# A recurrence with one PSUM bank per pair of heads, r-times-state beside U, and the state carried on VectorE

## The chip, the cores and the metric

The kernel runs on one core of a Trainium2 chip. The metric is device time in microseconds (us) of one execution, the median of several. One core has a matrix engine (TensorE, "PE" in the profile, with its weight loads as "PEld"), VectorE ("DVE"), ScalarE ("ACT"), GpSimd ("POOL") and SyncE ("SP"), which here issues the transfers. Matrix products write to PSUM, which has eight banks of 2 KiB per partition; VectorE and ScalarE read it from there.

## The reference, cut to what matters

One decoder layer: RMSNorm with modulation, one input projection, an RWKV-7 time-mixing group (8 heads of 64), a latent-attention group (8 heads), gates, an output projection, a final RMSNorm. SEQ is 1024, D_MODEL 1024, everything in f32. The change concerns the recurrence of the time-mixing group alone:

```python
def rwkv7_scan(r, w, k, v, kk, a):
    def step(state, inp):
        r_t, w_t, k_t, v_t, kk_t, a_t = inp
        sa = jnp.einsum('bhvk,bhk->bhv', state, kk_t)
        state = (state * w_t[:, :, None, :]
                 - sa[..., None] * (kk_t * a_t)[:, :, None, :]
                 + v_t[..., None] * k_t[:, :, None, :])
        y = jnp.einsum('bhvk,bhk->bhv', state, r_t)
        return state, y
    s0 = jnp.zeros((B, H, N, N), jnp.float32)
    _, ys = lax.scan(step, s0, xs)
    return jnp.moveaxis(ys, 0, 1)
```

## The kernel before

The tokens are cut into 16 chunks of 64. Inside a chunk the recurrence is written with matrices; from chunk to chunk a 64 x 64 state per head is handed on. Heads are taken in pairs: two heads share the 128 partitions (64 rows each, index `s`), and two pairs (index `a`) are worked on together, so a group of four heads has 16 chunks one after the other, and there are two such groups. Four chunks of a group make a *unit*; there are eight units, 0 to 3 for the first group and 4 to 7 for the second.

For each unit, `prep`, `products`, `invert`, `fetch` and `tmat` make the matrices: `GA` (the products of keys and queries inside a chunk, for U and for the outputs), `TT` (the inverse of a triangular matrix, whose 31 steps of two operations each run on VectorE, lines L625 and L627), `KB` (keys, turned), `rq` (queries scaled by decays) and `eL` (the decay over a whole chunk). `chain` then runs the recurrence, chunk by chunk, with three stages for each chunk, separated by `yield`:

1. X: four products of `GA` with `ST` (L694) into PSUM, and a ScalarE copy to `X` (L697). `ST` holds, for each chunk and head, the state in one half of the partitions and the values v in the other.
2. U: four products of `TT` with `X` (L701), and two ScalarE operations that write -U in the place of the state in `ST` (L703, L704).
3. State and output. State: for each pair an identity product with the old state `Sv` (L709) and a product of `KB` with `ST` on top of it (L712) in the same PSUM place; then ScalarE scales the sum by `eL` and writes it four times into the next chunk's `ST` (L720) and twice into `Sn` (L722). Output: a product of `rq` with the old state (L725) and one of `GA` with `ST` on top (L728), into `Y`.

X, U and next state of both pairs lie in one bank (tag `rc`), the outputs `Y` of all four chunks in another (`ry`). `post` copies `Y` out when the unit is done (L739) and norms, gates and stores it.

The outer loop at the end of the listing walks the units; unit `n` is prepared while `n - 1` is inverted and `n - 2` is in `chain`. `STEPS` gives the number of places for each unit, and every second place runs one stage of `chain`. Between them `filler` puts the input projection's products (`mm3`, lines L164 to L166: three products of 128 x 512 for each contraction tile, `RATE` of these triples per place), and later those of the values. A list scheduler then sets the final order on each engine by priorities and by its own estimate of when an operation can start; `quick` raises the priority of the recurrence's evacuations. Each engine works its queue in that order, and an operation that waits holds up all behind it. A product that reuses a bank, and an evacuation of it, wait for each other.

`acc`, at the start of the kernel, takes six banks for the first three projection tiles, and uses the two banks of `rc` and `ry` for one of them.

Of the kernel before, what the change touches and what calls it, by code (L numbers as in the profile page):

```python
# [17 lines left out]
F32 = mybir.dt.float32  # L18
# [68 lines left out]
def hymba_kernel(ctx: ExitStack, tc: tile.TileContext, x, pos, cols, cst, winit, w_ada, b_gate, w_in, w_lora, w0,  # L87
# [157 lines left out]
    with ExitStack() as s0:  # L245
# [62 lines left out]
        for i in range(4, 8):  # L308
            load_x(i)
        ws.append(load_w(GROUP[2][0], P, st, 3, st))  # L310
        acc = [[(psM if m == 0 else psA).tile([P, HALF], F32, tag=t, name=f"acc{m}{h}", bufs=1 if m == 1 else 2)
                for h, t in enumerate(tags)] for m, tags in enumerate((("mm", "mm"), ("rc", "ry"), ("rt", "rt")))]
# [365 lines left out]
    def chain(un, nxt):  # L678
# [8 lines left out]
        ps = psA.tile([P, 3, 2, C], F32, tag="rc", name="rc", bufs=1)  # L687
        Y = un["Y"] = psA.tile([P, 8, C], F32, tag="ry", name="Y", bufs=1)
        for i in range(4):
            last = i == 3 and nxt is None  # L690
            cc = [a * 4 + i for a in range(2)]
            for a in range(2):
                for s in range(2):
                    T.matmul(ps[rows[s], 0, a, :], lhsT=GA[s][a][:, i, 0:C], rhs=ST[:, cc[a], s, :], start=True, stop=True)  # L694
            X = ch.tile([P, 2, C], F32, tag="X", name="X", bufs=2)
            with quick(un):
                A.copy(X[:], ps[:, 0])  # L697
            yield
            for a in range(2):
                for s in range(2):  # L700
                    T.matmul(ps[rows[s], 1, a, :], lhsT=TT[rows[s], cc[a], :], rhs=X[rows[s], a, :], start=True, stop=True)  # L701
            with quick(un):
                A.mul(ST[lo, i:8:4, 0, :], ps[lo, 1], -1.0)  # L703
                A.mul(ST[hi, i:8:4, 1, :], ps[hi, 1], -1.0)  # L704
            yield
            Sn = None if last else ch.tile([P, 2, C], F32, tag="S", name="S", bufs=2)
            for a in range(0 if last else 2):
                for s in range(2 if Sv else 0):
                    T.matmul(ps[rows[s], 2, a, :], lhsT=ident[rows[s], rows[s]], rhs=Sv[rows[s], a, :],  # L709
                             start=True, stop=False)  # L710
                for s in range(2):
                    T.matmul(ps[rows[s], 2, a, :], lhsT=KB[:, s, cc[a], :], rhs=ST[:, cc[a], s, :],  # L712
                             start=Sv is None, stop=True)
            if not last:

                dst, n = (ST, i + 1) if i < 3 else (nxt["ST"], 0)
                with quick(un):
                    for a in range(2):
                        for s in range(2):
                            A.mul(dst[rows[s], a * 4 + n, s, :], ps[rows[s], 2, a, :], eL[rows[s], cc[a]:cc[a] + 1])  # L720
                    for a in range(2):
                        A.mul(Sn[:, a], ps[:, 2, a], eL[:, cc[a]:cc[a] + 1])  # L722
# [653 lines left out]
```

## Time and profile before

| | us |
|---|---|
| median of 3 runs | 940.63 |
| lowest and highest | 936.82, 945.03 |
| the profiled execution | 940.97 |
| its span, first to last instruction | 939.0 |
| first to last recurrence product | 176 to 628 |

A row of a timeline has start, duration, engine, line, operation, tiles (written <- read) and a count of merged rows. A row of groups has the busy time, the mean time of one in ns, and behind the second bar the idle time of the engine just before and what ended it. In the names of shapes 64\*64 is rows x columns of the weights.

### The profile page before, as it was taken

The page shows a single profiled execution, that of the slowest core. Times are in us where ns is not written, and L with a number is a line of the kernel's source. Part 1 is how long each engine was busy: PE and PEld are TensorE (multiplying, and loading weights), DVE is VectorE, ACT ScalarE, POOL GpSimd, SP SyncE. Part 2 cuts the span into 40 slices and gives each one's busy share as a digit, 9 for nine tenths or more (in the row PEclk, how much of TensorE's full clock was granted, in tenths as well). Part 3 has the DMA queues.
Part 4 walks back from the last instruction along what each step waited for, and adds up shares of the span by engine and source line. Part 5 has one row for each costly group of instructions (what it writes and reads, how often), then busy time and mean ns, then how long its engine had stood idle before and what let it go on. Part 6 is the DMA issues. An engine that isn't in the chain of part 4 may idle for free.

```text
span 939.0 us, 16568 instructions
## 1 busy us (share of the span) xinstructions
PE 852.4 (91%) x5812; PEld 654.2 (70%) x5812; DVE 576.8 (61%) x1462; ACT 477.4 (51%) x1112; POOL 298.7 (32%) x351
## 2 busy tenths in 40 slices
PE   1798997999999999898999999997799998989797
PEld 1586785776777777566777767765678777868685
DVE  5795358376584836747558275266678878763333
ACT  3555231444646545355254564554678888872311
POOL 2311432132222413332151321243346454454300
PEclk9998998999999999997999889989799999999898
DMA  8764443424444434344324443165202121036133
GB/s 266 244 175 146 135 121 102 127 82 118 131 124 98 141 85 136 83 114 148 72 87 119 110 137 101 56 184 157 54 18 72 46 89 48 1 102 214 57 124 123
DMA packets 131714, 106.66 MB, mean 114 GB/s; under 512 B 40616, under 2 KB 108464, under 8 KB 131632
## 3 DMA queue, kind: packets, MB, share of 16 engines
q1 hardware_dynamic: 130672, 102.46, 37.1%
q0 software_dynamic: 960, 3.15, 1.4%
q8 instruction: 46, 0.75, 0.3%
q14 instruction: 36, 0.29, 0.1%
HBM read 76.46 MB, written 29.10 MB: 112 GB/s over the span
## 4 chain that ended last, share of the span: by engine, by line
PE 62%; DVE 14%; ACT 11%; DMA 5%; issue 4%; POOL 2%; SPq 1%; DVEq 0%; POOLq 0%; ACTq 0%
PE mm L164 10%; PE mm L165 8%; PE mm L166 8%; ACT pr L1082 3%; PE gps L577 2%; DMA wor<-in_w_out 2%; DVE wtmp L625 2%; ACT PTh L1102 2%; PE tp L1093 2%; DVE W L627 2%; PE po L1155 2%; PE po L1157 2%; PE po L1156 2%; PE rc L694 1%; PE Y L728 1%
## 5 line engine op out<-in xcount | busy, mean ns | idle before, releaser
L164 PE MATMUL mm<-hTh,whi 128*128 128x512 f32 (+1 forms) x384 | 169.5, 441 | 3.2 <-DVE wtmp L625 2.3
L166 PE MATMUL mm<-hTh,wlo 128*128 128x512 f32 (+1 forms) x384 | 158.7, 413 | 0.0
L165 PE MATMUL mm<-hTl,whi 128*128 128x512 f32 (+1 forms) x384 | 158.6, 413 | 0.0
L157 POOL TENSOR_TENSOR wlo<-wraw,whi 128x512 fp32r<-128x512 f32 (+1 forms) x54 | 71.5, 1326 | 237.3 <-ACT whi L156 218.8
L164 PEld LDWEIGHTS mm<-hTh,whi 128*128 128x128 f32 (+1 forms) x384 | 74.2, 193 | 24.4 <-issue 3.2
L166 PEld LDWEIGHTS mm<-hTh,wlo 128*128 128x128 f32 (+1 forms) x384 | 74.6, 194 | 18.3
L165 PEld LDWEIGHTS mm<-hTl,whi 128*128 128x128 f32 (+1 forms) x384 | 74.6, 194 | 14.9 <-issue 1.1
L1086 POOL TENSOR_SCALAR pr<-pr,sm 128x512 f32<-128x512 f32 (+2 forms) x96 | 56.0, 592 | 75.4 <-DVE sm L1083 56.3
L625 DVE TENSOR_TENSOR wtmp<-W,N 128x60 f32<-128x60 f32 (+24 forms) x248 | 69.4, 280 | 5.5
L627 DVE TENSOR_TENSOR W<-W,wtmp 128x60 f32<-128x60 f32 (+24 forms) x248 | 68.9, 278 | 5.8 <-DVE wtmp L625 0.3
L156 ACT CAST whi<-wraw 128x512 fp32r<-128x512 f32 (+1 forms) x54 | 32.6, 606 | 62.3 <-PE mm L165 37.4
L1082 ACT ACTIVATE pr<-sp,mx,rss 128x128 f32<-128x128 f32 (+3 forms) x64 | 53.4, 834 | 17.5 <-DVE mx L1075 15.3
L720 ACT ACTIVATE ST<-rc,eL 64x64 f32<-64x64 f32 x120 | 37.1, 309 | 46.7 <-PE rc L712 45.1
L1103 DVE TENSOR_TENSOR PTl<-tp,PTh 128x512 fp32r<-128x512 f32 (+2 forms) x96 | 52.4, 553 | 12.1 <-ACT PTh L1102 9.8
L1155 PE MATMUL po<-wo,yh 128*128 128x512 f32 x128 | 51.4, 402 | 5.6 <-DVE xo L1288 4.8
L1074 DVE TENSOR_REDUCE mx<-sp 128x1 f32<-128x128 f32 (+3 forms) x64 | 48.0, 750 | 12.5 <-PE sp L1068 12.4
L1102 ACT CAST PTh<-tp 128x512 fp32r<-128x512 f32 (+2 forms) x96 | 44.1, 478 | 16.1 <-PE tp L1093 12.4
L1157 PE MATMUL po<-wo,yl 128*128 128x512 f32 x128 | 50.9, 398 | 0.0
L1156 PE MATMUL po<-wo,yh 128*128 128x512 f32 x128 | 50.9, 398 | 0.0
L1093 PE MATMUL tp<-cstt,pr 128*128 128x128 f32 x288 | 45.5, 279 | 4.2 <-DVE PTl L1103 2.1
L1114 PE MATMUL op<-PTh,Vt 128*128 128x256 f32 (+1 forms) x160 | 42.2, 294 | 5.6 <-ACT od L1129 5.1
L1064 PE MATMUL sp<-kt,qt 96*128 96x512 f32 (+2 forms) x96 | 36.9, 384 | 6.5 <-ACT pr L1082 6.4
(279 smaller groups left out, 1945.8 us busy)
## 6 DMA issues: line engine op xcount, KB each, us to landing
wraw<-in_w_in SPq DMA_DIRECT2D x52, 256.0 KB, 3.2
wa<-in_w_ada SPq DMA_DIRECT2D x64, 128.0 KB, 3.1
xt<-in_x SPq DMA_DIRECT2D x8, 512.0 KB, 7.1
wg<-in_w_ada SPq DMA_DIRECT2D x32, 128.0 KB, 2.6
N<-d_n SPq DMA_DIRECT2D x32, 128.0 KB, 3.1
wor<-in_w_out SPq DMA_DIRECT2D x16, 256.0 KB, 3.0
cr<-d_c SPq DMA_DIRECT2D x14, 256.0 KB, 3.1
d_c<-craw SPq DMA_DIRECT2D x10, 256.0 KB, 2.9
```

Of the source, the lines that this page charges most:

```text
L157: G.tensor_tensor(lo[:, :, :m], raw[:, :, :m], hi[:, :, :m].bitcast(F32), ALU.subtract)
L164: T.matmul(ps[:m], lhsT=hi[:, k % 4, :m], rhs=a, start=first, stop=False)
L165: T.matmul(ps[:m], lhsT=hi[:, k % 4, :m], rhs=b, start=False, stop=False)
L166: T.matmul(ps[:m], lhsT=lo[:, k % 4, :m], rhs=a, start=False, stop=last)
L625: V.tensor_tensor(t, W[:, 0:n, u:u + 1].to_broadcast([P, n, m]), N[:, u:u + 1, u + 1:32].to_broadcast([P, n, m]), ALU.mult)
L627: V.tensor_tensor(W[:, 0:n, u + 1:32], W[:, 0:n, u + 1:32], t, ALU.subtract)
L1082: A.activation(pr[:, 0:n], sp[:, 0:n], AF.Exp, scale=rss[:, i:i + 1], bias=mx[:], accum_out=sm[:])
L1093: T.transpose(tp[:, j, :], pr[:, (j0 + j) * P:(j0 + j + 1) * P], ident)
L1102: A.copy(th[:, 0:m, bs], tp[:, 0:m])
L1155: T.matmul(ps, lhsT=yh[k][:, ts_], rhs=hi, start=first, stop=False)
L1156: T.matmul(ps, lhsT=yh[k][:, ts_], rhs=lo, start=False, stop=False)
L1157: T.matmul(ps, lhsT=yl[k][:, ts_], rhs=hi, start=False, stop=last)
```

## The change

The bank: one tile of two banks is taken once before the loop, one bank for each pair `a`, with eight places of 64 columns: X, U, next state, one unused, and the four chunks' outputs. The separate bank for `Y` is gone; `post` copies from places 4 to 7 (L744).

The outputs: the products of `rq` with the old state move from the third stage to the second, behind the U products (L706). In the third stage the products of `GA` with `ST` (L715) come first and those of `KB` (L719) behind them.

The state: the identity product is gone. VectorE computes `Sn` = PSUM x `eL` + `Se` for each pair (L729; L727 in the first chunk, without `Se`), ScalarE copies `Sn` twice into the next chunk's `ST` (L731), and GpSimd makes `Se`, the new state times the next chunk's decay, ahead of time (L734).

At the start of the kernel `acc` takes one tile of two banks where it took two tiles.

```diff
--- before.py
+++ after.py
@@ -308,8 +308,10 @@
         for i in range(4, 8):
             load_x(i)
         ws.append(load_w(GROUP[2][0], P, st, 3, st))
-        acc = [[(psM if m == 0 else psA).tile([P, HALF], F32, tag=t, name=f"acc{m}{h}", bufs=1 if m == 1 else 2)
-                for h, t in enumerate(tags)] for m, tags in enumerate((("mm", "mm"), ("rc", "ry"), ("rt", "rt")))]
+        acc = [[(psM if m == 0 else psA).tile([P, HALF], F32, tag="rt" if m else "mm", name=f"acc{m}{h}")
+                for h in range(2)] for m in (0, 2)]
+        both = psA.tile([P, 2, HALF], F32, tag="rc", name="acc1", bufs=1)
+        acc.insert(1, [both[:, h] for h in range(2)])
         seq = [(0, 0), (1, 0), (0, 1), (1, 1)] + [(kt, h) for kt in range(2, NK) for h in range(2)]
         modulation(0)
         turn_x(*seq[0])
@@ -684,59 +686,62 @@
         if Sv is None:
             G.memset(ST[0:64, 0:8:4, 0, :], 0.0)
             G.memset(ST[64:128, 0:8:4, 1, :], 0.0)
-        ps = psA.tile([P, 3, 2, C], F32, tag="rc", name="rc", bufs=1)
-        Y = un["Y"] = psA.tile([P, 8, C], F32, tag="ry", name="Y", bufs=1)
+        ps = un["Y"] = bank
+        Se = un.get("Se")
         for i in range(4):
             last = i == 3 and nxt is None
             cc = [a * 4 + i for a in range(2)]
             for a in range(2):
                 for s in range(2):
-                    T.matmul(ps[rows[s], 0, a, :], lhsT=GA[s][a][:, i, 0:C], rhs=ST[:, cc[a], s, :], start=True, stop=True)
+                    T.matmul(ps[rows[s], a, 0, :], lhsT=GA[s][a][:, i, 0:C], rhs=ST[:, cc[a], s, :], start=True, stop=True)
             X = ch.tile([P, 2, C], F32, tag="X", name="X", bufs=2)
             with quick(un):
-                A.copy(X[:], ps[:, 0])
+                A.copy(X[:], ps[:, :, 0])
             yield
             for a in range(2):
                 for s in range(2):
-                    T.matmul(ps[rows[s], 1, a, :], lhsT=TT[rows[s], cc[a], :], rhs=X[rows[s], a, :], start=True, stop=True)
+                    T.matmul(ps[rows[s], a, 1, :], lhsT=TT[rows[s], cc[a], :], rhs=X[rows[s], a, :], start=True, stop=True)
+            for a in range(2 if Sv else 0):
+                for s in range(2):
+                    T.matmul(ps[rows[s], a, 4 + i, :], lhsT=rq[rows[s], cc[a], 1, :], rhs=Sv[rows[s], a, :],
+                             start=True, stop=False)
             with quick(un):
-                A.mul(ST[lo, i:8:4, 0, :], ps[lo, 1], -1.0)
-                A.mul(ST[hi, i:8:4, 1, :], ps[hi, 1], -1.0)
+                A.mul(ST[lo, i:8:4, 0, :], ps[lo, :, 1], -1.0)
+                A.mul(ST[hi, i:8:4, 1, :], ps[hi, :, 1], -1.0)
             yield
             Sn = None if last else ch.tile([P, 2, C], F32, tag="S", name="S", bufs=2)
+            for a in range(2):
+                for s in range(2):
+                    T.matmul(ps[rows[s], a, 4 + i, :], lhsT=GA[s][a][:, i, C:2 * C], rhs=ST[:, cc[a], s, :],
+                             start=Sv is None, stop=True)
             for a in range(0 if last else 2):
-                for s in range(2 if Sv else 0):
-                    T.matmul(ps[rows[s], 2, a, :], lhsT=ident[rows[s], rows[s]], rhs=Sv[rows[s], a, :],
-                             start=True, stop=False)
                 for s in range(2):
-                    T.matmul(ps[rows[s], 2, a, :], lhsT=KB[:, s, cc[a], :], rhs=ST[:, cc[a], s, :],
-                             start=Sv is None, stop=True)
+                    T.matmul(ps[rows[s], a, 2, :], lhsT=KB[:, s, cc[a], :], rhs=ST[:, cc[a], s, :], start=True, stop=True)
             if not last:
 
-                dst, n = (ST, i + 1) if i < 3 else (nxt["ST"], 0)
+                dst, n, eN = (ST, i + 1, eL) if i < 3 else (nxt["ST"], 0, nxt["eL"])
                 with quick(un):
                     for a in range(2):
-                        for s in range(2):
-                            A.mul(dst[rows[s], a * 4 + n, s, :], ps[rows[s], 2, a, :], eL[rows[s], cc[a]:cc[a] + 1])
-                    for a in range(2):
-                        A.mul(Sn[:, a], ps[:, 2, a], eL[:, cc[a]:cc[a] + 1])
-            for a in range(2):
-                for s in range(2 if Sv else 0):
-                    T.matmul(Y[rows[s], cc[a], :], lhsT=rq[rows[s], cc[a], 1, :], rhs=Sv[rows[s], a, :],
-                             start=True, stop=False)
-                for s in range(2):
-                    T.matmul(Y[rows[s], cc[a], :], lhsT=GA[s][a][:, i, C:2 * C], rhs=ST[:, cc[a], s, :],
-                             start=Sv is None, stop=True)
+                        e1 = eL[:, cc[a]:cc[a] + 1]
+                        if Sv is None:
+                            V.tensor_scalar(Sn[:, a], ps[:, a, 2], e1, None, ALU.mult)
+                        else:
+                            V.scalar_tensor_tensor(Sn[:, a], ps[:, a, 2], e1, Se[:, a], ALU.mult, ALU.add)
+                    for s in range(2):
+                        A.copy(dst[rows[s], n:8:4, s, :], Sn[rows[s]])
+
+                Se = ch.tile([P, 2, C], F32, tag="Se", name="Se", bufs=2)
+                G.tensor_tensor(Se[:], Sn[:], eN[:, n:8:4][:, :, None].to_broadcast([P, 2, C]), ALU.mult)
             Sv = Sn
             if i == 3 and nxt:
-                nxt["S"] = Sv
+                nxt["S"], nxt["Se"] = Sv, Se
             yield
 
     def post(un):
 
         Y = un["Y"]
         ys = evp.tile([P, 8, C], F32, tag="p2", name="ys", bufs=2)
-        A.copy(ys[:], Y[:])
+        A.copy(ys[:].rearrange("p (a i) t -> p a i t", a=2), Y[:, :, 4:8])
         s1 = evp.tile([P, 8], F32, tag="s1", name="s1")
         V.tensor_reduce(s1[:], ys[:], AX.X, ALU.add)
         V.tensor_scalar(s1[:], s1[:], 1.0 / C, None, ALU.mult)
@@ -1003,6 +1008,8 @@
                 put(j, lambda g3=g3: next(g3, None))
         return at_
 
+
+    bank = psA.tile([P, 2, 8, C], F32, tag="rc", name="rc", bufs=1)
     turned, la = [], latents()
     fill = filler()
     debt = 0.0
```

PE's queue in the second chunk of unit 1, third stage, before. `mm` is a projection tile, `nps` a small sum for `prep`, `rc` and `Y` the recurrence's banks; x2 counts products:

```order
L166 MATMUL mm<-hTh_132,wlo 128x512
L709 MATMUL rc<-S,cstt 64x64 x2
L712 MATMUL rc<-ST,KB 64x64 x2
L709 MATMUL rc<-S,cstt 64x64 x2
L712 MATMUL rc<-ST,KB 64x64 x2
L725 MATMUL Y<-S,rq 64x64 x2
L728 MATMUL Y<-ST,GA 64x64 x2
L725 MATMUL Y<-S,rq 64x64 x2
L728 MATMUL Y<-ST,GA 64x64 x2
L509 MATMUL nps<-cstt,sq 128x2 x4
```

After, the second and the third stage of the same chunk, in two pieces (`aps` and `zps` are small projections for `prep`, `vps` turns values):

```order
L703 MATMUL rc<-X,TT_831 64x64 x4
L706 MATMUL rc<-S,rq 64x64 x4
L495 MATMUL aps<-LW,wl 128x256
L611 MATMUL vps<-cstt,v 64x128 x4
L497 MATMUL zps<-wl,LW 128x128 x2
```

```order
L166 MATMUL mm<-hTh_132,wlo 128x512
L715 MATMUL rc<-ST,GA 64x64 x4
L719 MATMUL rc<-ST,KB 64x64 x4
L511 MATMUL nps<-cstt,sq 128x2 x4
L164 MATMUL mm<-hTh_133,whi 128x512
```

The r-times-state products stand behind U, and the third stage is two groups of one shape where eight groups alternated.

ScalarE's queue around the state step of the third chunk of unit 5, before and after (`whi` is the upper part of a projection weight, `craw` and `csq` evacuate a projection tile):

```order
L703 ACTIVATE ST<-rc 64x2x64
L704 ACTIVATE ST<-rc 64x2x64
L357 COPY craw<-mm 128x512
L360 ACTIVATE csq<-mm 128x512
L720 ACTIVATE ST<-rc,eL 64x64 x4
L722 ACTIVATE S<-rc,eL 128x64 x2
L156 CAST whi<-wraw 128x512
L697 COPY X<-rc 128x128
```

```order
L709 ACTIVATE ST<-rc 64x2x64
L710 ACTIVATE ST<-rc 64x2x64
L156 CAST whi<-wraw 128x512
L359 COPY craw<-mm 128x512
L731 COPY ST<-S 64x2x64 x2
L362 ACTIVATE csq<-mm 128x512
L699 COPY X<-rc 128x128
L709 ACTIVATE ST<-rc 64x2x64
```

Six evacuations of the state have become two copies, and an evacuation stands on either side of them.

PE's queue in a chunk of unit 6 in which little other work lies between the stages, before and after (`ytps` turns outputs in `post`, `vps` turns values):

```order
L701 MATMUL rc<-X,TT_831 64x64 x4
L609 MATMUL vps<-cstt,v 64x128 x4
L728 MATMUL Y<-ST,GA 64x64
L709 MATMUL rc<-S,cstt 64x64 x2
L712 MATMUL rc<-ST,KB 64x64 x2
L709 MATMUL rc<-S,cstt 64x64 x2
L712 MATMUL rc<-ST,KB 64x64 x2
L728 MATMUL Y<-ST,GA 64x64
L725 MATMUL Y<-S,rq 64x64 x2
L728 MATMUL Y<-ST,GA 64x64 x2
L164 MATMUL mm<-hTh_130,whi 128x512
L165 MATMUL mm<-hTl_138,whi 128x512
```

```order
L696 MATMUL rc<-ST,GA 64x64 x4
L763 MATMUL ytps<-cstt,ys 64x128 x4
L703 MATMUL rc<-X,TT_830 64x64 x4
L706 MATMUL rc<-S,rq 64x64 x4
L715 MATMUL rc<-ST,GA 64x64 x4
L719 MATMUL rc<-ST,KB 64x64 x3
L611 MATMUL vps<-cstt,v 64x128 x4
L719 MATMUL rc<-ST,KB 64x64
L696 MATMUL rc<-ST,GA 64x64 x4
```

The X products of the next chunk now stand directly behind the last state product; before, the outputs and some projection products came between. VectorE's queue at the same chunk, after (`cql`, `wql` and `W` belong to a latent, a weight and the inversion, `tg` to a gate):

```order
L796 TENSOR_TENSOR wql<-wqr,wqh 128x128
L627 TENSOR_TENSOR wtmp<-W,N 128x63
L729 SCALAR_TENSOR_TENSOR S<-rc,eL,Se 128x64
L629 TENSOR_TENSOR W<-W,wtmp 128x3x21
L729 SCALAR_TENSOR_TENSOR S<-rc,eL,Se 128x64
L627 TENSOR_TENSOR wtmp<-W,N 128x60
L629 TENSOR_TENSOR W<-W,wtmp 128x3x20
```

The two new operations are parted by a step of the inversion.

## The prediction

> **What bounds the kernel now.** I read the page's engine shares first, then the windows view over the stretch in which the chunk recurrence runs (its first product starts at 176 us, its last ends at 628 us), then the chain of waits over that stretch.
>
> ```profile
> PE 852.4 (91%) x5812; PEld 654.2 (70%) x5812; DVE 576.8 (61%) x1462; ACT 477.4 (51%) x1112; POOL 298.7 (32%) x351
> ```
>
> ```profile
> 176.00:628.00 452.00, 437.38 (x3580) 318.05 (x3579) 266.00 (x763) 227.38 (x579) 127.93 (x118) 0.94 0.39 111
> ```
>
> The columns of the second row are the stretch, its length, then busy time of PE, PEld, DVE, ACT and POOL, then the granted clock. PE has work for 437.4 of 452 us; VectorE for 266, ScalarE for 227, GpSimd for 128. So PE is the bound, and what is removed from it there is worth its full time unless something else is late. The chain of waits over the same stretch says how much of the recurrence lies on the path:
>
> ```profile
> by line: PE mm L164 16.7%; PE mm L165 14.2%; PE mm L166 14.0%; PE gps L577 3.6%; PE rc L694 2.9%; PE rc L712 2.7%; PE Y L725 2.6%; PE Y L728 2.6%; PE rc L709 2.6%; PE rc L701 2.5%; DVE wtmp L625 2.5%; DVE W L627 2.3%; PE lps L363 2.2%; issu
> ```
>
> The four groups of the state and output products (L709, L712, L725, L728) make 2.6 + 2.7 + 2.6 + 2.6 = 10.5% of 452 us, 47.5 us of path.
>
> **What one chunk's state and output products cost.** PE's timeline in a usual chunk. The profile writes each of these f32 products as two records, so x4 is two products:
>
> ```profile
> 309.87 0.33 PE L709 MATMUL rc<-S,cstt 64*64 64x64 f32 x4
> 310.13 0.34 PE L712 MATMUL rc<-ST,KB 128*64 128x64 f32 x4
> 310.40 0.33 PE L709 MATMUL rc<-S,cstt 64*64 64x64 f32 x4
> ...
> 311.71 0.34 PE L728 MATMUL Y<-ST,GA 128*64 128x64 f32 x4
> 311.98 1.05 PE L509 MATMUL nps<-cstt,sq 128*128 128x2 f32 x8
> ```
>
> Groups of 64-row and 128-row products alternate, and every four records take 0.26 to 0.27 us from start to start. The eight groups take 311.98 - 309.87 = 2.11 us. The first chunk of a group of heads has no state yet, so the identity and r-times-state products are left out there and equal shapes follow one another:
>
> ```profile
> 181.77 0.45 PE L712 MATMUL rc<-ST,KB 128*64 128x64 f32 x8
> 182.05 0.40 PE L728 MATMUL Y<-ST,GA 128*64 128x64 f32 x8
> 182.39 0.50 PE L164 MATMUL mm<-hTh,whi 128*128 128x512 f32 x1
> ```
>
> Eight records take 0.28 us, eight more 0.34 with the step to the next shape: 0.62 us together. In the one place where r-times-state stands straight behind the U products, of the same 64-row shape, I read:
>
> ```profile
> 591.97 0.45 PE L701 MATMUL rc<-X,TT 64*64 64x64 f32 x8
> 592.25 0.28 PE L725 MATMUL Y<-S,rq 64*64 64x64 f32 x4
> 592.54 0.50 PE L164 MATMUL mm<-hTh,whi 128*128 128x512 f32 x1
> ```
>
> Eight records behind an equal shape take 0.28 us. This place is the price of the moved r-times-state products. The alternation, more than the number of products, makes the 2.11 us.
>
> **The change part by part, on PE.** Two groups of heads with 16 chunks each make 32 chunks. Before: 28 chunks of 2.11 us, the 2 first ones of 0.62 and the 2 last ones (no next state) of about half of 2.11: 59.1 + 1.2 + 2.1 = 62.4 us. After, the order shows outputs and state products back to back in nearly every chunk, both of 128 rows: 30 x 0.62 + 2 x 0.31 = 19.2 us. The r-times-state products of 30 chunks move behind U: 30 x 0.28 = 8.4 us. PE loses 62.4 - 27.6 = 34.8 us of work. The X products are cut by a projection product in a few more chunks than before, which stays within the waits below. Of the 62.4 us, 47.5 (76%) lay on the chain of waits, so the gain on the path lies between 0.76 x 34.8 = 26.5 and 34.8 us. PE was idle for only 14.6 of 452 us, which is nearer to the upper end: I take 31.
>
> **On the other engines.** Durations from the groups by shape:
>
> ```profile
> L720 ACT ACTIVATE ST<-rc,eL 64x64 f32<-64x64 f32 x120 | 37.1, 309 | 46.7 <-PE rc L712 45.1
> ...
> L722 ACT ACTIVATE S<-rc,eL 128x64 f32<-128x64 f32 x60 | 15.9, 311 | 0.8
> ...
> L212 DVE SCALAR_TENSOR_TENSOR pst<-mm,colt,pst 128x511 f32<-128x511 f32 x20 | 14.9, 746 | 33.7 <-ACT pst L211 33.7
> ...
> L1131 POOL TENSOR_TENSOR oc<-oc,od 128x256 f32<-128x256 f32 x16 | 11.8, 740 | 9.3 <-ACT od L1129 9.2
> ...
> L697 ACT COPY X<-rc 128x128 f32<-128x128 f32 x32 | 8.5, 265 | 20.2 <-PE rc L694 20.0
> ...
> L539 DVE SCALAR_TENSOR_TENSOR kn<-k,colt,kps 128x256 f32<-128x256 f32 x16 | 7.5, 470 | 7.1 <-PE kps L536 7.1
> ```
>
> ScalarE loses 120 x 0.309 + 60 x 0.311 = 55.7 us and gets 60 copies of 128 columns at 0.265: 15.9. It isn't the bound, so this is costed at nothing. VectorE gets 60 operations on 64 columns of a PSUM bank; between L539 and L212 a column costs (746 - 470) / 255 = 1.08 ns, so 470 - 192 x 1.08 = 263 ns, 15.8 us in all on an engine with 186 us free in the stretch. GpSimd gets 30 products of 128 columns: half to all of L1131's 740 ns, I take 0.5 us, 15 us in all; each result is wanted only one chunk later (452 / 32 = 14 us).
>
> **The wait that could take the place.** The next chunk's X products wait for the new state. This is VectorE's, GpSimd's, ScalarE's and PE's timeline around one state step, and then ScalarE's and PE's in a tight one:
>
> ```profile
> 320.25 2.64 POOL L547 TENSOR_TENSOR kb<-kw,Ei 64x512 f32<-64x512 f32 x2
> ...
> 320.37 1.23 DVE L627 TENSOR_TENSOR W<-W,wtmp 128x60 f32<-128x60 f32 x1
> ...
> 325.12 1.29 ACT L720 ACTIVATE ST<-rc,eL 64x64 f32<-64x64 f32 x4 [3.10 <-PE rc L712]
> ...
> 325.57 0.20 DVE L627 TENSOR_TENSOR W<-W,wtmp 128x48 f32<-128x48 f32 x1
> ...
> 329.37 0.45 PE L694 MATMUL rc<-ST,GA 128*64 128x64 f32 x8
> ```
>
> ```profile
> 615.35 1.29 ACT L720 ACTIVATE ST<-rc,eL 64x64 f32<-64x64 f32 x4 [1.22 <-PE rc L712]
> ...
> 617.44 0.69 PE L694 MATMUL rc<-ST,GA 128*64 128x64 f32 x8
> ```
>
> Before: 1.29 + 2 x 0.31 = 1.91 us on ScalarE alone. After: 2 x 0.263 on VectorE, then 2 x 0.265 on ScalarE, 1.06 us and one more handover, if VectorE is free. It isn't always: the new operations stand in its queue among the inversion's steps and evacuations, sometimes with one or more between the pair's halves. A step takes 0.20 us at 325.57 but 1.23 beside GpSimd's product at 320.25, so I reckon with 2 to 3 us for the hop. In the usual chunk, 329.37 - 325.12 = 4.25 us pass before the X products come up, and nobody waits. In the tight one it is 2.09. By the order some six of 30 chunks have under 2 us of PE work behind the state products, and in the chunk that the section on the change shows last there is almost none. Before, such waits were small:
>
> ```profile
> PE Y L725 <- ACT S L722: 2.4, 2, 1.3
> ```
>
> Six chunks at 1 to 2 us, less the 2.4 us already paid and about as much again hidden under it, make +4. Bounds: 0 if the hop stays as long as it was, 15 us if half of the 30 chunks wait 1 us each. Queued behind a waiting VectorE operation are evacuations of projection tiles, on which PE's next projection may wait; that is in the 15. The outputs' bank is now written two stages earlier in a unit, behind the copy that empties it; also in the 15.
>
> GpSimd's extra products stretch VectorE's inversion steps, as at 320.37: 1 us, bounds 0 and 6 (30 x 0.2). A rule of the Trainium skill speaks against the change here, in "SBUF — State Buffer", section "Who interferes with whom": a VectorE instruction with two SBUF inputs and a GpSimd instruction that reads SBUF exclude each other, the later one waits for the whole of the other. The row at 320.37 agrees. By the rule alone, with each new GpSimd product in front of such a step, it would be 30 x 0.5 = 15 us of VectorE time, and the sum below 14 us higher if all of it lay on the path.
>
> The granted clock:
>
> ```profile
> 309.00:313.00 4.00, 4.00 (x46) 3.01 (x45) 3.92 (x14) 3.00 (x9) 1.79 (x1) 1.00 0.56 179
> 313.00:316.40 3.40, 3.40 (x10) 2.60 (x9) 3.16 (x11) 0.62 (x1) 2.69 (x2) 0.50 0.30 78
> ```
>
> The block above and the eight tiny products behind it (309.87 to 313) are followed by 3.4 us at half clock. Over the 452 us the clock is 0.94, a loss of 27 us. Shorter blocks of small products may spare some: -2, bounds -13 (half of the loss) and +5 (new idle places do the same).
>
> **The sum**, against the profiled execution's own 940.97 us, which stands 0.3 above the median of the runs: 940.97 - 31 + 4 + 1 - 2 = 913.0 us.
>
> **The rivals.**
> 1. Only the identity goes. If a record costs the same in any order, the change saves 28 x 2 x 0.26 = 14.6 us, less 5 for the new waits: 931. The pure groups at 181.77 speak against it; two places only, both beside little other work, speak for caution.
> 2. The clock. If the half-speed stretches follow blocks of small products as at 313, thinning the blocks gives 11 us more: 902 to 900. For it speaks the row; against it that other half-speed stretches may have other causes. The Trainium skill has such a rule in "TensorE: Matmul & The Clock Gate", Part 1: activity over windows of about 3.4 us releases or closes the gate; the row's 3.4 us agrees.
> 3. Slower: the state stands behind VectorE's queue. Each of the new operations waits for PE in order, and ahead of some stand evacuations that themselves wait for ScalarE:
>
> ```profile
> DVE tg L233 <- ACT tg L232: 28.1, 7, 6.9
> ```
>
> That is 4 us each. If all 30 chunks met one, the hop would be 5 us against 4.25 of cover in the usual chunk and 2.09 in a tight one. It decides from 1.25 us of PE wait per chunk on average beyond my sum (28 + 9.4 us over 30 chunks); at 1.5 us the time is 913 + 45 = 958. Against it: evacuations are 7 such waits in the whole stretch.
> 4. No change: the chain through VectorE (the inversion's L625 and L627, 4.8% of the path) takes over as PE gets shorter, and the gain shrinks to under 9 us: about 936. Against it: VectorE has 186 us free.
>
> **How the numbers follow.** The forecast's own case (901 to 926) 0.60; rival 1 0.13; rival 2 0.11; rival 3 0.07; rival 4 0.09. The time is the likeliest case's, 913. The range 898 to 932 takes in rivals 1 and 2 and leaves out 3 and 4, with the tails. About 1% (9.4 us) is what a measurement of this kernel can tell from no change. Faster by over 1% (under 931.2): 0.60 + 0.11 + most of rival 1, 0.81. Slower by over 1%: 0.07. Within 1%: 0.12.
>
> **What would show it.** In the changed profile: outputs and state products as two groups of x8 within 0.6 to 0.65 us; r-times-state behind U in 0.28 us; PE's busy time shorter by some 33 us; the stretch from the first to the last chunk product near 425 us; VectorE's new operation near 260 ns; X products waiting for the ScalarE copies for under 10 us in all; the clock at or above 0.94. I would be wrong if mixed groups remained at 0.26 us per four records, if X waited for 1 us or more in most chunks, or if GpSimd's product came late for VectorE.

## The result and the profile after

The changed kernel takes 950.45 us (median of 10 runs, 942.62 to 958.42) against 938.73 us before (10 runs, 930.54 to 946.38): a ratio of 1.0123, 95% interval 1.008 to 1.0166. It became about 1.2% slower, where 3% faster was forecast. Its profiled execution took 952.62 us, the span is 950.8. (Medians, here and below, are over all runs and ratios leave disturbed ones out, so that the two don't always quite agree.)

First the engine shares of the whole span, the stretch of the recurrence before and after (after: first product at 174, last end at 638; columns as in the prediction), and the chain of waits over that stretch:

```profile
PE 840.0 (88%) x5588; PEld 650.0 (68%) x5588; DVE 587.3 (62%) x1522; ACT 444.9 (47%) x992; POOL 309.2 (33%) x381
```

```profile
176.00:628.50 452.50, 437.88 (x3585) 318.36 (x3584) 266.50 (x764) 227.68 (x579) 127.93 (x118) 0.94 0.39 111
174.00:638.00 464.00, 426.84 (x3361) 316.09 (x3360) 277.32 (x826) 195.41 (x460) 140.38 (x149) 0.89 0.38 109
```

```profile
by line: PE mm L164 12.5%; PE mm L165 11.1%; PE mm L166 10.7%; DVE wtmp L627 5.0%; DVE W L629 4.7%; PE gps L579 4.1%; issue 3.0%; PE rc L696 2.4%; PE rc L703 2.1%; PE lps L365 2.0%; PE tps L601 1.7%; PE ytps L763 1.5%; PE rc L715 1.5%; POOL
```

The stretch has three parts that can be read from its row: idle time of TensorE is length less PE busy; what half clock costs is length x (1 - PEclk); the rest is work at full clock.

| the recurrence's stretch, us | before (176 to 628.5) | after |
|---|---|---|
| length | 452.5 | 464.0 |
| TensorE idle | 14.6 | 37.2 |
| lost to half clock (two digits of PEclk: within 2 or 3 us) | 27 | 51 |
| work at full clock, the rest | 411 | 376 |

So 35 us of TensorE's work did go, and 23 us of idle time and 24 us of half clock came: +12, which is the whole difference of the spans (939.0 to 950.8). The chain of waits says where the idle time comes from: the inversion's two lines on VectorE have risen from 2.5% and 2.3% to 5.0% and 4.7%.

The products themselves look as forecast. TensorE's timeline of a chunk with no cut:

```profile
307.25 0.45 PE L703 MATMUL rc<-X,TT 64*64 64x64 f32 x8
307.53 0.40 PE L706 MATMUL rc<-S,rq 64*64 64x64 f32 x8
307.86 0.71 PE L601 MATMUL tps<-cstt,kb 64*128 64x64 f32 x8
308.66 0.45 PE L715 MATMUL rc<-ST,GA 128*64 128x64 f32 x8
308.94 0.40 PE L719 MATMUL rc<-ST,KB 128*64 128x64 f32 x8
309.27 0.63 PE L611 MATMUL vps<-cstt,v 128*64 128x128 f32 x4
```

Outputs and state take 309.27 - 308.66 = 0.61 us, r times state 0.33. TensorE's waits in the stretch, the longest (engine, line, what it waited for; us in all, times, longest):

```profile
PE ytps L763 <- POOL ys L756: 6.9, 5, 2.1
PE rc L696 <- ACT ST L731: 5.4, 4, 3.6
PE gps L579 <- DVE wtmp L627: 5.1, 2, 2.7
PE gps L579 <- DVE W L629: 5.1, 2, 3.8
PE rc L715 <- ACT ST L710: 3.7, 5, 0.8
PE mm L164 <- DVE cr L394: 3.0, 1, 3.0
PE gps L579 <- DVE GA L586: 2.7, 1, 2.7
```

The new state is late for X (L696) for 5.4 us in all. Most of the rest is other work: the products of the next unit (`gps`) wait for VectorE, 12.9 us, and the turns of finished outputs (`ytps`) for GpSimd, 6.9. Before, no wait in the stretch was above 2.4 us in all. One of the waits for `gps`, on TensorE and then on VectorE:

```profile
514.18 0.39 PE L165 MATMUL mm<-hTl,whi 128*128 128x512 f32 x1
514.41 0.40 PE L166 MATMUL mm<-hTh,wlo 128*128 128x512 f32 x1
517.52 2.39 PE L579 MATMUL gps<-rq,kb 64*128 64x128 f32 x12 [2.71 <-DVE GA L586]
```

```profile
511.60 0.23 DVE L627 TENSOR_TENSOR wtmp<-W,N 128x69 f32<-128x69 f32 x1
511.86 0.23 DVE L629 TENSOR_TENSOR W<-W,wtmp 128x69 f32<-128x69 f32 x1
...
515.18 0.48 DVE L941 SCALAR_TENSOR_TENSOR ag<-wg,csil,ag 128x256 f32<-128x256 f32 x1
515.58 1.29 DVE L629 TENSOR_TENSOR W<-W,wtmp 128x72 f32<-128x72 f32 x1
516.79 0.68 DVE L586 TENSOR_TENSOR GA<-gps,cstt 128x512 f32<-128x512 f32 x1
```

VectorE is busy all through these 5 us: it works off inversion steps and other evacuations, and the evacuation of the first products (L586), which frees the bank for the next ones, stands behind them. TensorE has run ahead of VectorE's queue. One of these steps takes 1.29 us where the others take 0.23; it runs beside this product on GpSimd:

```profile
515.31 1.47 POOL L157 TENSOR_TENSOR wlo<-wraw,whi 128x512 fp32r<-128x512 f32 x1 [4.05 <-ACT whi L156]
```

The idle place is followed by half clock. The windows around another such wait, 206.8 to 209.18:

```profile
203.00:206.80 3.80, 3.78 (x29) 2.56 (x28) 3.80 (x9) 0.16 (x1) 2.13 (x2) 1.00 0.09 32
206.80:209.18 2.38, 0.00 (x1) 0.03 (x1) 2.37 (x7) 0.53 (x1) 0.11 (x1) 1.00 0.14 46
209.18:216.00 6.82, 6.82 (x29) 5.10 (x30) 6.53 (x25) 0.59 (x2) 0.40 (x1) 0.50 0.22 64
216.00:220.00 4.00, 4.00 (x46) 2.95 (x42) 1.80 (x10) 2.53 (x5) 1.04 (x1) 0.99 0.02 8
```

TensorE stands for 2.38 us, VectorE works through them, and then TensorE runs for 6.8 us at half clock: the wait costs 2.4 us of standing, and 3.4 us of slowness follow it.

### The profile page after: what moved, and what is told of

It reads as the page before. It is cut to its first block, busy times and chain, and to the rows that moved or that the text cites. A ratio compares the mean times of both kernels' runs of the same rounds, so it can differ in the third digit from the quotient of the medians.

```text
span 950.8 us, 16103 instructions
## 1 busy us (share of the span) xinstructions
PE 840.0 (88%) x5588; PEld 650.0 (68%) x5588; DVE 587.3 (62%) x1522; ACT 444.9 (47%) x992; POOL 309.2 (33%) x381
## 4 chain that ended last, share of the span: by engine, by line
PE 50%; DVE 20%; ACT 10%; DMA 9%; issue 5%; POOL 5%; SPq 1%; DVEq 0%; POOLq 0%; ACTq 0%
PE mm L164 8%; PE mm L165 7%; PE mm L166 7%; DVE wtmp L627 3%; DVE W L629 3%; PE gps L579 3%; ACT pr L1089 3%; DMA wor<-in_w_out 2%; PE tp L1100 2%; ACT PTh L1109 2%; PE po L1162 2%; PE po L1163 2%; PE po L1164 2%; PE rc L696 1%; POOL wor L1155 1%
## 5 line engine op out<-in xcount | busy, mean ns | idle before, releaser
L165 PE MATMUL mm<-hTl,whi 128*128 128x512 f32 (+1 forms) x384 | 160.6, 418 | 0.0
L157 POOL TENSOR_TENSOR wlo<-wraw,whi 128x512 fp32r<-128x512 f32 (+1 forms) x54 | 69.4, 1285 | 219.2 <-ACT whi L156 214.6
L627 DVE TENSOR_TENSOR wtmp<-W,N 128x60 f32<-128x60 f32 (+24 forms) x248 | 72.8, 294 | 5.1
L579 PE MATMUL gps<-rq,kb 64*128 64x128 f32 x256 | 31.3, 329 | 20.3 <-DVE W L629 10.7
L579 PEld LDWEIGHTS gps<-rq,kb 64*128 64x128 f32 x256 | 26.1, 220 | 28.1 <-issue 19.6
```

The source lines that it names most:

```text
L157: G.tensor_tensor(lo[:, :, :m], raw[:, :, :m], hi[:, :, :m].bitcast(F32), ALU.subtract)
L165: T.matmul(ps[:m], lhsT=hi[:, k % 4, :m], rhs=b, start=False, stop=False)
L579: T.matmul(pp[s][:, i, :], lhsT=kb[rows, c, :, :].rearrange("p a t -> p (a t)"), rhs=rq[rows, c, :, :].rearrange("p a t -> p (a t)"), star ...
L627: V.tensor_tensor(t, W[:, 0:n, u:u + 1].to_broadcast([P, n, m]), N[:, u:u + 1, u + 1:32].to_broadcast([P, n, m]), ALU.mult)
```

## The experiments

The theories, as the expectations name them. A: the carry through VectorE's queue gives back what TensorE saves. B: VectorE's queue, with the inversion in it, is the next bound whatever carries the state. C: the new order and banks cost by themselves. D: `Se`, waiting at the head of GpSimd's queue, holds up what is behind it. E: the waits come from the order or the clock alone. F: an earlier prep is worth as much in either kernel. G: a wait that is taken away comes back at the next place. Ratios are to the kernel before, in runs on the same chip, with 95% intervals; the batches' own medians of the kernel before lay between 935.5 and 939.3 us, so close calls go by the ratio.

| run | us | ratio (interval) |
|---|---|---|
| e1_identity_back | 947.91 | 1.0101 (1.0055 to 1.0146) |
| e2_carry_alone | 943.54 | 1.0064 (1.0025 to 1.0103) |
| e3_se_scalar | 939.46 | 0.9981 (0.9944 to 1.0018) |
| e4_state_not_quick | 946.86 | 1.0113 (1.0072 to 1.0154) |
| i1_before_half_inverse | 917.07 | 0.978 (0.9691 to 0.9869) |
| i2_after_half_inverse | 903.32 | 0.9635 (0.957 to 0.97) |
| i3_order_half_inverse | 904.44 | 0.9668 (0.9582 to 0.9753) |
| i4_se_scalar_half_inverse | 898.45 | 0.9604 (0.9526 to 0.9682) |
| f1_products_first | 937.38 | 1.0008 (0.9972 to 1.0045) |
| f2_prep_earlier | 930.88 | 0.994 (0.9903 to 0.9977) |
| g0_before_prep_earlier | 929.55 | 0.9911 (0.9879 to 0.9942) |
| g1_prep_and_post | 931.25 | 0.9921 (0.989 to 0.9952) |
| g2_after_prep_earlier | 943.75 | 1.0052 (1.0024 to 1.008) |
| h3_carry_scalar_old_order | 935.43 | 0.9938 (0.9882 to 0.9993) |
| k1_se_later | 951.21 | 1.0181 (1.0081 to 1.0281) |
| d1_dummy_waits | 947.15 | 1.0124 (1.0036 to 1.0212) |
| d2_dummy_free | 946.13 | 1.0098 (1.0056 to 1.014) |
| r1_relieved | 935.15 | 0.9986 (0.9951 to 1.0021) |

### The change in parts

**The carry undone.** The changed kernel with the identity product and ScalarE's evacuation back:

```diff
             for a in range(0 if last else 2):
+                for s in range(2 if Sv else 0):
+                    T.matmul(ps[rows[s], a, 2, :], lhsT=ident[rows[s], rows[s]], rhs=Sv[rows[s], a, :],
+                             start=True, stop=False)
...
-                            V.scalar_tensor_tensor(Sn[:, a], ps[:, a, 2], e1, Se[:, a], ALU.mult, ALU.add)
+                            A.mul(dst[rows[s], a * 4 + n, s, :], ps[rows[s], a, 2, :], eL[rows[s], cc[a]:cc[a] + 1])
```

> The changed kernel with one part undone: the identity product is back behind the r-times-state and output products, the state is evacuated by ScalarE's six multiplications, and nothing of the carry is on VectorE or GpSimd; a bank per pair, r times state beside U and the homogeneous order of products stay. Theory A (the carry through VectorE's queue gives back what TensorE saves): TensorE's saving shrinks from 30 us to about 18 us, but VectorE's 25 us of waits for rc and TensorE's 18 us of waits for W, wtmp and GA go back to the 12 us of before, so 915 to 928 us. Rival B (VectorE's inversion is the next bound whatever carries the state): TensorE catches up with it all the same, 932 to 945 us. Rival C (the other order of products and the bank per pair are to blame): 945 us or more.

947.91 us: as slow as the changed kernel. Theory A falls: without any carry on VectorE, what TensorE saves is given back too. By the figure alone C has it (945 us or more) and B's bracket is missed by 3 us; the runs with half an inversion, below, decide between these two. Its stretch:

```profile
172.50:638.70 466.20, 432.64 (x3605) 319.57 (x3604) 271.38 (x775) 229.02 (x584) 128.04 (x119) 0.92 0.38 110
```

33.6 us idle and 37 lost to the clock leave 396 of work, 15 less than before; the stretch is 14 longer.

**The carry alone,** in the kernel before:

> The kernel before with the carry alone: no identity product, the state by VectorE and copied twice by ScalarE, Se by GpSimd; the old banks and the old order of the products, alternating between the two shapes. Theory A: TensorE loses some 7 to 10 us of products, VectorE waits for the product as in the changed kernel (20 us or more in all), and the time is 945 to 965 us, slower than before. Rival B: the carry costs nothing by itself and TensorE's shorter chain is hidden: 930 to 942 us. Rival C (banks and order to blame): 925 to 935 us.

943.54 us, between the sides. The carry by itself, with `Se` on GpSimd, loses 0.6%, less than theory A wants.

**Se on ScalarE:**

```diff
-                G.tensor_tensor(Se[:], Sn[:], eN[:, n:8:4][:, :, None].to_broadcast([P, 2, C]), ALU.mult)
+                for a in range(2):
+                    A.mul(Se[:, a], Sn[:, a], eN[:, a * 4 + n:a * 4 + n + 1])
```

> The changed kernel with the product Se (old state times next decay) made by two multiplications on ScalarE in place of one on GpSimd. Theory D (Se at the head of GpSimd's queue, 50 us of waits, makes ys late and TensorE wait for it 7 us): GpSimd's wait for S goes, TensorE's for ys falls under 2 us, 938 to 945 us. Theory A: GpSimd's queue is not what costs; 947 to 955 us, VectorE's waits for rc as they were (about 25 us).

939.46 us, the kernel before's own time: 11 us better than the change as made. That is theory D's figure, but TensorE's wait for `ys` only fell from 6.9 to 5.8 us; what the price is made of is taken up below. Against the run with the identity back (0.9981 to 1.0101) the carry by VectorE gains 1.2%.

**VectorE's two instructions without raised priority** (they were taken out of `quick`):

> The changed kernel with VectorE's two state instructions taken out of the raised priority, so that the order puts other VectorE work ahead of them; the two copies of ScalarE stay raised. Theory A, head of the queue: VectorE's wait for rc falls from 25 us to under 10 us, TensorE's waits for W, wtmp and GA with it, and the time falls to 930 to 942 us, unless the state itself comes later: then TensorE's waits for ST and X grow and it stays at 945 to 955 us. Rival B: no change, 947 to 953 us.

946.86 us, and nothing is learned from it: VectorE's wait for the state product stayed, since only four of the 60 instructions changed their place in VectorE's queue, each by two.

```profile
DVE S L728 <- PE rc L719: 21.8, 10, 3.5
```

### VectorE relieved

**Half of the inversion.** The same edit in four kernels: before, changed, changed with the identity back, changed with `Se` on ScalarE. It leaves out 15 of the 31 steps, so these runs tell of time alone.

```diff
-        for u in range(31):
+        for u in range(0, 31, 2):
```

> The kernel before with 16 of the 31 inversion steps (every second one; the others are left out, so the inverse is not the full one), which takes about half of the inversion's work off VectorE's queue. Theory B (VectorE's queue, with the inversion between the steps of prep and products, is the next bound): TensorE bounds the kernel before, so it gains only its few waits for W, wtmp and kb: 925 to 938 us. Theory E (TensorE's waits come from the order alone): the same. It is the base line of the next run.

> The changed kernel with the same 16 of 31 inversion steps, the others left out. Theory B: with VectorE's queue relieved TensorE's saving comes through; the waits for W, wtmp and GA (13 us in the chain's stretch) and much of the 24 us of extra half clock go, so 15 to 35 us below the kernel before with the same cut, 900 to 920 us. Theory E (the order, or the clock by itself): no gain against that kernel, or a loss as with the full inversion: 930 to 950 us.

> The run without the carry (identity back, new banks and order) with 16 of 31 inversion steps, the others left out; base line is the kernel before with the same cut, 917 us. Theory B (VectorE's queue hides the saving): of the 18 us that TensorE's products get shorter at least half comes through, 900 to 909 us. Rival C (the new order costs by itself): 917 to 927 us, as it costs 9 us with the full inversion.

> The changed kernel with Se on ScalarE and 16 of 31 inversion steps, the others left out; base line is the changed kernel with the same cut, 903 us. If Se on GpSimd costs the same whatever VectorE does: 890 to 895 us. If it costs only while VectorE is the bound: 900 to 905 us.

| medians, us | full inversion | half | what the half saves |
|---|---|---|---|
| before | 938.7 | 917.1 | 22 |
| changed | 950.5 | 903.3 | 47 |
| changed, identity back | 947.9 | 904.4 | 43 |
| changed, Se on ScalarE | 939.5 | 898.5 | 41 |

With the full inversion the three changed kernels are behind the kernel before by 12 and 9 us and level with it; with the half one they are 14, 13 and 19 us ahead of it (0.985, 0.989 and 0.982 as ratios; each interval reaches some 0.012 to either side, so that of the second, taken alone, just reaches no change). Theory B gives the sign in all three. C falls, for the order and banks that lost 1% gain 1% once VectorE is relieved, a turn of 2.2% that is clear of both intervals; and E falls, which asked for 930 us or more of the changed kernel. The stretches of before and after with the half inversion:

```profile
170.70:608.00 437.30, 425.39 (x3565) 309.15 (x3564) 216.30 (x553) 227.28 (x578) 128.81 (x119) 0.96 0.40 115
```

```profile
171.10:591.20 420.10, 398.31 (x3342) 293.60 (x3341) 239.70 (x615) 196.19 (x461) 141.96 (x150) 0.94 0.42 121
```

Idle time goes from 11.9 to 21.8 us where it went from 14.6 to 37.2, and the clock from 0.96 to 0.94 where it went from 0.94 to 0.89. The waits of `gps` for W, wtmp and GA are gone from the head of the list; those that lead it are others:

```profile
PE ytps L763 <- POOL ys L756: 5.0, 3, 2.0
PE rc L715 <- ACT ST L710: 3.5, 4, 1.7
PE nps L511 <- DVE z L500: 2.7, 3, 1.7
```

Two figures of the expectations were missed. The kernel before gained 22 us itself, where its visible waits for VectorE promised only a few; and the changed kernel, though at 903 inside its bracket, is 14 us ahead of its base line and not 15 to 35. `i4` fell between its two sides (898.45): `Se` on GpSimd costs 5 us there by the medians and 3 by the ratios, within the intervals of nothing.

**Products ahead of the inversion.** With `Se` on ScalarE, the last four steps of prep and the evacuation of `gps` put under a priority raised by 120:

> The changed kernel with Se on ScalarE, and with VectorE's last four steps of prep and its evacuation of the products (GA) raised in priority, ahead of the inversion steps. Theory B: TensorE's waits for W, wtmp and GA (15 us with Se on ScalarE) fall under 6 us; 922 to 934 us, unless the inversion then comes late and TensorE waits in its place for T or TT. Theory E: 936 to 943 us.

937.38 us, a miss. Its waits in the stretch show why: those of the products for W, wtmp and GA are still 10.8 us, under one name, where they were 14.8 without the raised priority and were to fall under 6.

```profile
PE gps L580 <- DVE wtmp L629: 10.8, 4, 3.3
PE ytps L766 <- POOL ys L759: 7.5, 5, 2.3
```

**Prep two places earlier,** in the changed kernel with `Se` on ScalarE, in the kernel before, and in the changed kernel as it is:

```diff
-PREP = ((0, 0, 1, 2, 3, 15, 15), (4, 4, 5, 6, 7, 13, 13), (9, 9, 10, 11, 12, 14, 14), (0, 0, 1, 2, 3, 5, 5))
+PREP = ((0, 0, 1, 2, 3, 13, 13), (4, 4, 5, 6, 7, 11, 11), (9, 9, 10, 11, 12, 12, 13), (0, 0, 1, 2, 3, 5, 5))
```

> The changed kernel with Se on ScalarE, and with the last steps of prep put two places earlier in each unit, so that VectorE has two places more of TensorE's work to make kb before the products want it. Theory B: the waits of the products for W and wtmp (10 us) fall to about half, 930 to 937 us. Theory E: 937 to 945 us.

> The kernel before with the last steps of prep put two places earlier, as in the run before it: the control of that run. Theory B (the change moved the bound to VectorE's queue, and the earlier prep relieves that): the kernel before waits only 3 us for kb and wtmp, so 934 to 941 us, within 0.5%. Theory F (the earlier prep is worth as much in either kernel): 928 to 933 us.

> The changed kernel as it is, Se on GpSimd, with the earlier prep alone. If the step to ScalarE and the earlier prep are worth what they were singly (11 us and 8.5 us): 940 to 944 us. If the earlier prep alone relieves VectorE's queue and Se on GpSimd is then hidden: 930 to 935 us. If Se holds up GpSimd's queue whatever the order: 943 us or more.

930.88, 929.55 and 943.75 us. The control decides against B's reading of this edit: the earlier prep is worth 0.9% in the kernel before (theory F), where it shortens the half clock (0.96 of full speed in the stretch against 0.94), 0.4% in the changed kernel with `Se` on ScalarE and 0.7% in the changed kernel. It isn't evidence for B. And `Se` on GpSimd costs 1.1% (1.0052 to 0.994) in this order too.

**The outputs' turns three places later,** on top of the earlier prep (`POST` from 5, 5, 8 to 8, 8, 11):

> The changed kernel with Se on ScalarE, prep earlier, and the turns of the finished outputs (ytps) three places later, so that GpSimd's two steps on ys are done when TensorE comes to them. Theory B, next wait: TensorE's 5.6 us of waits for ys go, and some half clock behind them: 921 to 928 us. Rival G: the waits are only put off, to rc and gps, 929 to 933 us.

931.25 us, nothing gained, as rival G had it: no wait for `ys` is left among the first, and those for VectorE have grown in its place.

```profile
PE gps L579 <- DVE W L629: 6.0, 2, 3.3
PE gps L579 <- DVE wtmp L627: 4.3, 1, 4.3
PE rc L696 <- ACT ST L731: 4.1, 3, 2.0
PE mm L164 <- DVE wtmp L627: 3.1, 1, 3.1
```

**Three small steps moved from VectorE to ScalarE** (L521, L659, L668), on top of the earlier prep:

> The changed kernel with Se on ScalarE and the earlier prep, and with three small steps of prep and tmat moved from VectorE to ScalarE: about 11 us of VectorE's work in all. Theory B: a share of TensorE's saving comes through, 920 to 928 us; if a VectorE relief this small changes nothing, or ScalarE's steps come late in their place: 929 to 935 us.

935.15 us, a miss: VectorE's busy time in the stretch fell by 9 us (275 to 267) and nothing came of it; the products' waits for W and wtmp were 9.4 us where they were 7.5.

**The parts added up:** old order and banks, carry with `Se` on ScalarE, earlier prep:

> The old banks and order of products, with the carry (no identity product, state by VectorE), Se on ScalarE and the earlier prep. If the effects found add up (carry alone +5 us, Se off GpSimd -11 us, earlier prep -8 us): 921 to 927 us. If the earlier prep has used up what there was to gain: 928 to 934 us.

935.43 us, ratio 0.9938, where adding them up asked for 0.985 or so (the expected 921 to 927 us): they don't add up. With the full inversion no version got past the kernel before with earlier prep (0.9911); the changed kernel with `Se` on ScalarE, prep and turns moved is level with it (0.9921).

### What Se on GpSimd costs

**Se later.** Its line was put behind the next chunk's U:

> The changed kernel with Se still on GpSimd, but put into the order one and a half chunk stages later, behind the next chunk's U, when the state it reads is long there. Theory D (Se waits at the head of GpSimd's queue and holds up what is behind it): GpSimd's 50 us of waits for S fall under 15 us and 938 to 944 us are reached, as with Se on ScalarE. If its price is something else (the operation itself, or VectorE slowed beside it): 946 to 954 us.

951.21 us, but the edit didn't reach what it was meant for: the list scheduler put the product where it had been, and GpSimd waited as before.

```profile
POOL Se L712 <- DVE S L731: 47.9, 16, 13.7
```

**An operation beside it.** `Se` stays on ScalarE, and GpSimd gets one operation of the same size, once reading the new state, once a constant:

```diff
+                Sd = ch.tile([P, 2, C], F32, tag="Sd", name="Sd", bufs=2)
+                G.tensor_tensor(Sd[:], Sn[:], eN[:, n:8:4][:, :, None].to_broadcast([P, 2, C]), ALU.mult)
```

> The changed kernel with Se on ScalarE, and besides an operation on GpSimd of Se's size that reads the new state and the decay, and whose result nobody reads. Theory D (the wait at the head of GpSimd's queue costs): 946 to 952 us, as with Se itself on GpSimd. If what costs is that the next state waits for GpSimd's result: 937 to 942 us.

> The same with the extra operation reading a constant and the decay, so that it never waits for the state; its result is not read either. Theory D: 937 to 942 us, as without it. If the operation itself costs (VectorE slowed beside it, or GpSimd's time): 946 to 952 us.

947.15 and 946.13 us: both lose 7 to 8 us against the run without it (939.46), 1.4% and 1.2% by the ratios. The second one never waits (the tile's view lists no release that it waited for) and nobody waits for it:

```profile
L737 POOL TENSOR_TENSOR Sd<-cstt,eL x30: 392/402/850, 92.8 to 496.6; 128x128 f32<-128x128 f32 x30
its engine sat idle before it (us, times) until:
who waited for it (us, times):
```

So it is neither the wait in GpSimd's queue (D falls) nor the state's waiting for GpSimd, but that thirty such operations of 0.40 us are there. The order is no rival in these two runs: in their traces TensorE, VectorE and ScalarE run the same instructions in the same order as without the extra operation, and GpSimd's order differs by the thirty alone.

By what way they cost 7 to 11 us isn't settled. In the changed kernel's trace the 29 inversion steps that run beside an `Se` take 0.31 us in the mean against 0.21 for those beside nothing on GpSimd, 29 x 0.10 = 3 us. The rule of the Trainium skill, "SBUF — State Buffer", section "Who interferes with whom", led to an estimate of 15 in the prediction; the rows beside an `Se` agree in the direction and not in the size. All inversion steps together are longer by more, 133.8 us without the extra operation and 142.6 with it:

```profile
L627 DVE TENSOR_TENSOR wtmp<-W,N 128x60 f32<-128x60 f32 (+24 forms) x248 | 68.8, 278 | 4.9
L629 DVE TENSOR_TENSOR W<-W,wtmp 128x60 f32<-128x60 f32 (+24 forms) x248 | 65.0, 262 | 5.1
```

```profile
L627 DVE TENSOR_TENSOR wtmp<-W,N 128x60 f32<-128x60 f32 (+24 forms) x248 | 73.7, 297 | 4.9
L629 DVE TENSOR_TENSOR W<-W,wtmp 128x60 f32<-128x60 f32 (+24 forms) x248 | 68.9, 278 | 5.1
```

These are the kernel with `Se` on ScalarE (e3) and the one with the operation that never waits (d2). The 9 us are of the size of the price, but they come from one profiled execution of each, and these two executions differ by only 1.5 us in their spans (939.5 and 941.0).

## Why the prediction was wrong

**TensorE's work: right.** Outputs and state were to take 0.62 us and take 0.61; r times state 0.28, takes 0.33; in all 34.8 us less, measured 411 - 376 = 35.

**The step that failed** is the next one: "PE was idle for only 14.6 of 452 us, which is nearer to the upper end: I take 31". Idle time before doesn't bound idle time after. Of the 35 us, 23 turned into standing, and the runs with half an inversion show for whom: with it each of the three changed kernels was ahead of the kernel before, without it behind or level. In the prediction this is rival 4, put at 0.09 and turned away with "VectorE has 186 us free". Those were free microseconds of the wrong kind: in the 5 us before 516.79 VectorE had none. The rival's price (no change, 936) was too mild as well, since it left out what a stall does to the clock.

**The clock: the sign was wrong.** -2 was reckoned, with a bound of +5 for "new idle places"; it was +24. The -2 by itself came about, and the bound was what failed. The stretches of half clock inside the recurrence in the two profiled executions, by the longest standstill of TensorE in the 4.5 us before each (us lost: half of the time at half clock):

| longest standstill before it | before: stretches, us lost | after: stretches, us lost |
|---|---|---|
| over 2 us | 1, 3.4 | 6, 22.1 |
| 1 to 2 us | 2, 5.1 | 3, 18.7 |
| 0.5 to 1 us | 2, 10.2 | 2, 5.1 |
| none | 3, 6.8 | 1, 3.4 |

Rival 2's reading, that half clock follows blocks of small products, has no standstill against it in the last line alone, as at 313 before. This line went down as forecast, by 3 us, and it held 7 us in all, too little for rival 2's 11. In all 20 traces, from 170 us on, half clock set in between the start of a standstill of over 2 us and 4.5 us after its end in 129 of 142 cases, for one of 1 to 2 us in 61 of 171, for one of 0.5 to 1 us in 75 of 337 (standstills that began at full clock); from a random moment at full clock it sets in within 5.5 us one time in ten. That idle places bring it on is read from this, and not tried by itself. The Trainium skill, "TensorE: Matmul & The Clock Gate", Part 1, lets the clock fall to half after an idle window of about 3.4 us. The length of the slow stretch in the row above, 6.82 us, agrees with two such windows; the standstill before it does not, since 2.38 us were enough, and there the measurement decides.

**The new waits of X: right in size.** +4 reckoned, 5.4 us measured (L696 for ST), and the hop itself is as reckoned:

```profile
L731 ACT COPY ST<-S 64x128 f32<-64x128 f32 x60 | 17.8, 296 | 51.7 <-DVE S L729 49.2 <-DVE S L727 1.5
...
L729 DVE SCALAR_TENSOR_TENSOR S<-rc,eL,Se 128x64 f32<-128x64 f32 x56 | 14.7, 277 | 26.4 <-PE rc L719 22.0 <-ACT pst L211 1.9 <-POOL ys L748 1.6
...
L734 POOL TENSOR_TENSOR Se<-S,eL 128x128 f32<-128x128 f32 x30 | 13.6, 453 | 68.6 <-DVE S L729 49.6 <-DVE wtmp L627 10.7 <-PE gps L579 3.8
```

277 ns against 263 forecast, 296 against 265, 453 against 500. Rival 3, the state behind VectorE's queue, was not it: the changed kernel with the identity back has no such queue and is as slow.

**GpSimd's products: mis-sized.** 1 us was reckoned, with 6 as the upper bound, for stretched inversion steps; taken off GpSimd the kernel is 11 us faster, and an idle copy of the operation costs 7 to 8. The steps beside an `Se` are longer by 3 us together, and how the rest comes about is open. The sum therefore missed in three terms: the idle time (+23 for +4, 5 of it the X waits), the clock (+24 for -2) and, inside these two, GpSimd's operations.

**Still open:** which share of VectorE's load matters. Halving the inversion shortened both its queue and the chain of dependent steps, and the smaller reliefs (f1, r1) gained nothing, so it may be the chain's length rather than VectorE's busy time. Part of that load is GpSimd's doing: in the changed kernel's trace all 36 inversion steps of over 0.9 us, which make 43 of the 142.5 us of the 496 steps, run beside a GpSimd instruction, most of them beside L157 or L549, and no step that ran beside none took over 0.24 us (before: 32 such steps, 39 us). No run moved that work. And of 35 us only 14 to 19 came through even then; `ytps` behind GpSimd and the outputs behind ScalarE's U were next.

## What to carry to other kernels

Before costing work taken off the busiest engine at its full time, ask at each place where that engine meets another's queue how far the other is ahead there, not how much free time it has in the mean: an engine that got 8% shorter here ran into a queue with 40% free time. Price a new standstill of TensorE at its length and the half clock behind it. To learn whether a saving is hidden or false, make the same cut in the suspected next engine in both kernels and compare the differences.

## What the runs showed of the hardware that was not expected

A standstill of TensorE of 2.4 us was followed by 6.8 us at half clock, which cost another 3.4 us (the rows at 206.8 and 209.18). Thirty operations of 0.40 us on GpSimd that wait for nothing and that nobody waits for made the kernel 7 us slower (946.13 to 939.46), with the order on TensorE, VectorE and ScalarE unchanged.
